# Six output tiles instead of four side by side in the first projection of a two-layer encoder step

## Chip, cores and metric

One Trainium2 chip, one core. The metric is device microseconds of one execution; of several runs the median counts.

## What is computed

One inference step of a two-layer streaming encoder, for 256 new frames of a prompt and 32 of a running stream, which the kernel keeps side by side as T = 288 columns. Layer 0 mixes tokens with a gated linear recurrence, layer 1 with differential attention; a gated convolutional MLP follows each. The change lies in layer 0's first part:

```python
def rglru_mixer(x, conv_hist, h0, w_in, conv_w, conv_b, gate_w, gate_b, log_lam, w_out):
    u = x @ w_in                                   # x is the RMS-normed input, 2048 wide; w_in 2048 x 4096
    gate_br, rec = u[..., :D_RNN], u[..., D_RNN:]
    y = jax.nn.gelu(gate_br)
    full = jnp.concatenate([conv_hist, rec], axis=1)
    xc = causal_dwconv(full, conv_w, conv_b, t)    # width 4
    g = sigmoid(einsum('btnc,ncd->btnd', xc.reshape(bsz, t, 16, 128), gate_w) + gate_b)
    r, i = g[..., :128], g[..., 128:]
    log_a = -8.0 * r * softplus(-log_lam)
    a, mult = exp(log_a), sqrt(-expm1(2.0 * log_a))
    h = linear_recurrence(a, mult * i * xc, h0)    # h[t] = a[t] * h[t-1] + b[t]
    return (h * y) @ w_out
```

## The kernel before, in words

Everything is fp32 and transposed: channels on the 128 partitions, the 288 columns along the free axis. A product of fp32 accuracy is made of three matmuls: high half of the weights by high half of the input (L926), high weights by low input (L927), low weights by high input (L928). ScalarE (ACT) makes each high half by a copy (weights L809, x L144), VectorE (DVE) each low half by a subtraction (weights L814, x L147). One 128-row chunk of one output tile is a triplet of such matmuls. Weights are streamed from HBM once.

The work is a list of units. A unit is some consecutive chunks (2, 4 or 8) of one output tile's weights: one load, one cut into halves, then its triplets. `phase(tiles, group)` (L224) orders the units of a stage: the first `group` tiles advance side by side, unit by unit, the rest come one after another. The first projection (L705 to L712) has 32 tiles: r0 to r15 feed the recurrence, g0 to g15 the gelu gate, in the order r0 r1 g0 g1 r2 r3, then r4 r5 g2 g3, r6 r7 g4 g5 and so on. Tiles with n below 2, which are the four of the group, are cut into units of 2, 2, 4 and 8 chunks, all others into 8 and 8. So units 0 to 3 need chunks 0 and 1 of x, units 4 to 7 chunks 2 and 3, units 8 to 11 chunks 4 to 7, units 12 to 15 chunks 8 to 15.

The order of the work on every engine is written out by the loop at L898, one step for each unit i: it loads units up to i + 5 (L804, on SyncE's queue SP), lets ACT cut unit i + 3 (four buffers, so this cut waits until TensorE has finished unit i - 1), runs all pending jobs that are due at i (`S.run_due`, L906), lets DVE write the low half of unit i + 3, and issues unit i's matmuls. Jobs due at the same step run in the order in which they were put on the list. All engines work their own instructions in order.

Before the loop, SP is given the constants (L856), the first twelve unit loads and the 16 x tiles, one transfer for each, in between (L857 to L862). Splits of later x tiles (L883), squares (L885), the norm row (L887) and other loads are jobs with due steps. The norm row (`norm_row`, L196) sums the squares by two matmuls with a matrix of ones: L198 for the sum that GpSimd (POOL) built (L167), L199 for the one that DVE built (L163). DVE then makes 1/sqrt by iteration (L176 to L191). Every tile's result waits for this row.

When a tile of the first projection is finished, its `rec_done` (L283) or `gate_done` (L376) puts a chain of jobs on the list:

- r tiles: s1 loads the raw gate weights (L274), copies three history columns (POOL, L291), scales the sums out of PSUM (DVE, L294 and L295) and applies the first tap (ACT, L297); s2 the other three taps (DVE, L304); s3 and s4 split the result and the gate weights (ACT L309 and L140, DVE L141 and L314); s6 the six gate matmuls (L326 to L328); s7 sigmoids and tanh (ACT, L334 to L339) and a product (POOL, L340); s8 a reciprocal (DVE, L343) and a product (POOL, L344); s9 a copy (L348). After each second tile, s10 takes square roots for both (ACT L357, products on POOL L358), and s11 runs the recurrence as two scans (DVE, L364 and L366).
- g tiles: scale (DVE, L207), gelu (ACT, L386), product with h (POOL, L389), split into Hh and Hl (L392, L395).

A stage's due step is the chain's base plus a lag. Before, the base is the tile's last unit i (i + 1 for r0 and r1) and a small extra w delays s6 and later for r0 to r3 (L350 to L373). Gelu, sqrt and the sigmoid and tanh pair use different ACT tables, each change of which is an ACT_TABLE_LOAD.

PSUM: four banks rotate among the tiles, a pair of banks (`psS`) serves the gates of even r tiles, two more (`psA`) the gates of odd ones and the norm.

## Time and profile before

| | us |
|---|---|
| median of 3 runs (2511.88 to 2512.2) | 2511.97 |
| the profiled execution | 2512.42 |
| its span, first to last instruction | 2510.6 |
| TensorE matmul busy (share of the span) | 2480.7 (99%) |
| VectorE busy | 1633.6 (65%) |
| ScalarE busy | 1198.4 (48%) |
| GpSimd busy | 282.7 (11%) |

Busy times are sums over the span; the engine names PE, PEld (weight load), DVE, ACT, POOL and SP are those of the profile. A row of a list in order of time gives the start, the duration, the engine, the source line, the operation, output and inputs with shapes, and in brackets the idle time before it with what ended it. The time of a matmul in the profile is a modelled one that overlaps the next matmul's; the distance between starts is the pace. The first projection runs from 5 to about 220 us.

### The profile page before, as it was taken

How to read it: one execution, taken by the hardware profiler on the slowest of the kernel's cores; microseconds unless marked ns; L12 is line 12 of the kernel's file. 1: busy time of each engine (PE TensorE's matmuls, PEld its weight loads, DVE VectorE, ACT ScalarE, POOL GpSimd, SP SyncE). 2: the span in 40 equal slices, each digit the busy share in tenths (PEclk: the TensorE clock that was granted, in tenths of full speed). 3: DMA queues.
4: the chain of work that ended last, by engine and by line, in shares of the span. 5: the costliest groups of instructions: out<-in, count | busy, mean ns of one | idle time of the engine just before them, and what ended most of it. 6: DMA issues, size and time to landing. Idle time of an engine off the chain costs nothing.

```text
span 2510.6 us, 46015 instructions
## 1 busy us (share of the span) xinstructions
PE 2480.7 (99%) x18556; PEld 2472.7 (98%) x18556; DVE 1633.6 (65%) x2599; ACT 1198.4 (48%) x1756; POOL 282.7 (11%) x779
## 2 busy tenths in 40 slices
PE   8999999999999999999999999999999999999997
PEld 7999999999999999999999999999999999999997
DVE  7987666666446666555677677766666446666544
ACT  6887444444334444444445444544444334444442
POOL 3554110000000000011000000210000000000011
PEclk9999999999999999999999999999999999999999
DMA  6444544445554444555554553544445554444553
GB/s 218 160 167 164 170 160 168 163 166 161 164 167 166 166 167 162 160 168 171 181 163 160 177 170 116 193 162 166 165 163 161 166 169 168 162 167 166 162 164 113
DMA packets 126934, 414.36 MB, mean 165 GB/s; under 512 B 14336, under 2 KB 24192, under 8 KB 126720
## 3 DMA queue, kind: packets, MB, share of 16 engines
q1 hardware_dynamic: 126288, 411.17, 49.8%
q8 instruction: 145, 2.38, 0.4%
q14 instruction: 69, 0.57, 0.1%
q10 hardware_dynamic: 432, 0.25, 0.0%
HBM read 403.86 MB, written 7.50 MB: 164 GB/s over the span
## 4 chain that ended last, share of the span: by engine, by line
PE 97%; DVE 1%; DMA 0%; issue 0%; ACT 0%; SPq 0%; DVEq 0%; ACTq 0%
PE acc L926 32%; PE acc L928 31%; PE acc L927 31%; DVE x L936 0%; DVE wl L814 0%; PE os_ps L653 0%; DMA wr<-w_in 0%; DMA x<-x 0%; PE spare L926 0%; PE gate_ps L327 0%; PE gate_ps L328 0%; PE spare L928 0%; PE spare L927 0%; PE gate_ps L326 0%; PE osq_ps L682 0%
## 5 line engine op out<-in xcount | busy, mean ns | idle before, releaser
L809 ACT ACTIVATE wh<-wr 128x1024 fp32r<-128x1024 f32 (+2 forms) x776 | 799.2, 1030 | 1206.2 <-PE acc L927 848.7
L814 DVE TENSOR_TENSOR wl<-wr,wh 128x1024 fp32r<-128x1024 f32 (+2 forms) x776 | 925.9, 1194 | 510.6 <-ACT wh L809 510.0
L926 PE MATMUL acc<-xh,wh 128*128 128x288 f32 x4096 | 1217.3, 297 | 5.0 <-ACT xh L144 5.0
L928 PE MATMUL acc<-xh,wl 128*128 128x288 f32 x4096 | 1206.4, 295 | 5.5 <-DVE wl L814 5.4
L927 PE MATMUL acc<-xl,wh 128*128 128x288 f32 x4096 | 1209.7, 295 | 0.0
L928 PEld LDWEIGHTS acc<-xh,wl 128*128 128x128 f32 x4096 | 772.3, 189 | 7.0 <-DVE wl L814 6.9
L926 PEld LDWEIGHTS acc<-xh,wh 128*128 128x128 f32 x4096 | 768.9, 188 | 5.7 <-ACT xh L144 5.0
L927 PEld LDWEIGHTS acc<-xl,wh 128*128 128x128 f32 x4096 | 770.1, 188 | 0.9 <-DVE xl L147 0.3
L927 PE MATMUL acc<-Hl,wh 128*128 128x288 f32 x1504 | 443.9, 295 | 0.8 <-DVE Hl L395 0.8
L926 PE MATMUL acc<-Hh,wh 128*128 128x288 f32 x1504 | 444.3, 295 | 0.0
L928 PE MATMUL acc<-Hh,wl 128*128 128x288 f32 x1504 | 442.9, 294 | 0.0
L927 PEld LDWEIGHTS acc<-Hl,wh 128*128 128x128 f32 x1504 | 282.3, 188 | 1.3 <-DVE Hl L395 1.3
L928 PEld LDWEIGHTS acc<-Hh,wl 128*128 128x128 f32 x1504 | 283.0, 188 | 0.0
L926 PEld LDWEIGHTS acc<-Hh,wh 128*128 128x128 f32 x1504 | 281.8, 187 | 0.1
L437 DVE SCALAR_TENSOR_TENSOR c<-up,cff,c 128x290 f32<-128x290 f32 x352 | 182.6, 519 | 6.2
L431 POOL COPY st_ff<-up 128x2 f32<-128x2 f32 x176 | 34.6, 197 | 1339.1 <-DVE up L427 1339.1
L426 DVE TENSOR_TENSOR up<-acc,rb 128x32 f32<-128x32 f32 x176 | 33.7, 191 | 128.7 <-PE acc L928 128.7
L926 PE MATMUL acc<-Hhx,wh 128*128 128x288 f32 x384 | 113.7, 296 | 0.0
L927 PE MATMUL acc<-Hlx,wh 128*128 128x288 f32 x384 | 113.3, 295 | 0.0
L928 PE MATMUL acc<-Hhx,wl 128*128 128x288 f32 x384 | 112.9, 294 | 0.0
L429 ACT ACTIVATE c<-up,cff 128x290 f32<-128x290 f32 x176 | 108.6, 617 | 0.7 <-DVE up L427 0.7
L167 POOL TENSOR_TENSOR ssq<-ssq,sq 128x288 f32<-128x288 f32 x63 | 70.1, 1113 | 288.9 <-ACT sq L154 288.4
(211 smaller groups left out, 1651.3 us busy)
## 6 DMA issues: line engine op xcount, KB each, us to landing
wr<-w_up SPq DMA_DIRECT2D x352, 512.0 KB, 3.7
wr<-w_dn SPq DMA_DIRECT2D x128, 448.0 KB, 3.3
wr<-w_qkv SPq DMA_DIRECT2D x96, 512.0 KB, 4.2
wr<-w_dn SPq DMA_DIRECT2D x64, 512.0 KB, 3.6
wr<-w_in SPq DMA_DIRECT2D x60, 512.0 KB, 3.9
wr<-w_rg_out SPq DMA_DIRECT2D x32, 512.0 KB, 3.7
wr<-w_at_out SPq DMA_DIRECT2D x24, 512.0 KB, 4.0
wr<-w_at_out SPq DMA_DIRECT2D x16, 256.0 KB, 3.1
```

Of the source, the lines that this page charges most:

```text
L167: nc.gpsimd.tensor_add(acc_box["a"], acc_box["a"], sq)
L426: nc.vector.tensor_mul(buf[:, 2:34], ps[:, 0:NS], rb[:, 0:NS])
L429: nc.scalar.activation(c, buf[:, 0:UP_N], AF.Identity, scale=ff(f"w{l}", f), bias=ff(f"b{l}", f))
L431: nc.gpsimd.tensor_copy(st_ff[:, f, 0, :], buf[:, 290:292])
L437: nc.vector.scalar_tensor_tensor(c, buf[:, t:t + UP_N], ff(f"w{l}", t * 2 * NF + f), c, op0=OP.mult, op1=OP.add)
L809: nc.scalar.activation(u["wh"][:, :n], u["raw"][:, :n], AF.Copy)
L814: nc.vector.tensor_sub(u["wl"][:, :n], u["raw"][:, :n], r32(u["wh"])[:, :n])
L926: nc.tensor.matmul(o, wh, h, start=u["first"] and z == 0, stop=False)
L927: nc.tensor.matmul(o, wh, lo, start=False, stop=False)
L928: nc.tensor.matmul(o, wl, h, start=False, stop=u["last"] and z == nk - 1)
```

## The change

- `FIRST = 6`: the six tiles r0 r1 g0 g1 r2 r3 advance side by side, all cut into 2, 2, 4 and 8. Units 0 to 5 need x chunks 0 and 1, units 6 to 11 chunks 2 and 3, units 12 to 17 chunks 4 to 7, units 18 to 23 chunks 8 to 15. Tiles 4 and 5 (r2, r3) accumulate in the two banks of `psS` (`bank` 0 and 1 of L913 to L919).
- x is loaded in eight transfers of two tiles each; the first 16 columns of the constants are loaded first, the rest after the second x pair; 16 units are loaded before the loop instead of 12.
- The coefficients (`coef`) become a job of step 8; splits, squares and the norm row move to later steps; so do the side loads, lambda and the state output.
- The chains of r0 to r5 get bases 21, 22, 23, 25, 25, 29 and extra lags w of 1, 2, 3, 3, 4, 2; for r2 to r5 s3 and s4 are delayed by w too.
- Buffers: three raw gate buffers instead of two, five `xc` and five `y` instead of four.

```diff
+FIRST = 6
-        raw = rgp.tile([P, 256], F32, tag="gwr", name="gwr")
+        raw = rgp.tile([P, 256], F32, tag="gwr", name="gwr", bufs=3)
-                e["xc"] = rgp.tile([P, REC_N], F32, tag="xc", name="xc", bufs=4)
+                e["xc"] = rgp.tile([P, REC_N], F32, tag="xc", name="xc", bufs=5)
-            w = (1, 2, 1, 1)[n] if n < 4 else 0
-            stages = [(1, s1), (2, s2), (3, s3), (4, s4)]
+            w = (1, 2, 3, 3, 4, 2)[n] if n < 6 else 0
+            v = w if n > 1 else 0
+            stages = [(1, s1), (2, s2), (3 + v, s3), (4 + v, s4)]
             stages += [(t + w, f) for t, f in ((6, s6), (7, s7), (8, s8), (9, s9))]
-            S.chain(i + (1 if n < 2 else 0), *stages)
+            S.chain((21, 22, 23, 25, 25, 29)[n] if n < 6 else i, *stages)
-                e["y"] = rgp.tile([P, T], F32, tag="y", name="y", bufs=4)
+                e["y"] = rgp.tile([P, T], F32, tag="y", name="y", bufs=5)
-    tiles = [tile_units(d["w_in"], n + (KC if w == "r" else 0), 0, [8, 8] if n >= 2 else [2, 2, 4, 8],
-                        xh, xl, need_of("n0"), rec_done(n) if w == "r" else gate_done(n))
-             for w, n in order]
-    phase(tiles, 4)
+    tiles = [tile_units(d["w_in"], n + (KC if w == "r" else 0), 0, [8, 8] if t >= FIRST else [2, 2, 4, 8],
+                        xh, xl, need_of("n0"), rec_done(n) if w == "r" else gate_done(n),
+                        t - 4 if t in (4, 5) else None)
+             for t, (w, n) in enumerate(order)]
+    phase(tiles, FIRST)
-    def load_x(a, b):
-        for c in range(a, b):
-            nc.sync.dma_start(x[c], d["x"][c // 2][:, (c % 2) * T:(c % 2 + 1) * T])
+    def load_x(*pairs):
+        for c in pairs:
+            nc.sync.dma_start(xx[c], d["x"][c])
-    nc.sync.dma_start(crg, d["p_rg"])
-    for i in range(12):
-        tag = "hs" if i < 4 else "y"
-        load(units[i], rgp.tile([P, T], F32, tag=tag, name="w0", bufs=4) if i < 8 else None)
-        if i in (0, 4, 8):
-            load_x(i // 2, max(i, 2))
-    load_x(8, KC)
+    nc.sync.dma_start(crg[:, 0:KC], d["p_rg"][:, 0:KC])
+    for i in range(16):
+        raw = None
+        if i < 2 * FIRST:
+            tag, n = (("hs", T), ("y", T), ("a", REC_N))[i // 4]
+            raw = rgp.tile([P, n], F32, tag=tag, name="w0", bufs=5 if tag == "y" else 4)
+        load(units[i], raw)
+        if i == 0:
+            load_x(0)
+        elif i == FIRST - 1:
+            load_x(1)
+            nc.sync.dma_start(crg[:, KC:], d["p_rg"][:, KC:])
+        elif i == 2 * FIRST - 1:
+            load_x(2, 3)
+    load_x(4, 5, 6, 7)
-    coef()
+    S.at(8, coef)
-    for t, c, n in ((1, 2, 2), (3, 4, 2), (5, 6, 2), (7, 8, 4), (8, 12, 4)):
+    for t, c, n in ((3, 2, 2), (9, 4, 2), (10, 6, 2), (14, 8, 4), (16, 12, 4)):
         S.at(t, lambda c=c, n=n: split_x(c, c + n))
-    for t, c, n in ((9, 0, 4), (10, 4, 4), (11, 8, 4), (12, 12, 4)):
+    for t, c, n in ((17, 0, 4), (18, 4, 4), (19, 8, 4), (20, 12, 4)):
         S.at(t, lambda c=c, n=n: square_x(c, c + n))
-    S.at(14, lambda: norm_row("n0"))
-    S.at(24, side_loads)
-    S.at(40, lam_setup)
+    S.at(21, lambda: norm_row("n0"))
+    S.at(28, side_loads)
+    S.at(44, lam_setup)
-    S.at(72 + 14, rg_states)
+    S.at(2 * 2 * KC + 2 * FIRST + 14, rg_states)
-    dma_ptr, cut_ptr = 12, 4
+    dma_ptr, cut_ptr = 16, 4
```

## Rows read from the trace of the kernel before

**Rows 1.** The page, parts 1 and 2: busy time of the engines, and TensorE's granted clock

```profile
PE 2480.7 (99%) x18556; PEld 2472.7 (98%) x18556; DVE 1633.6 (65%) x2599; ACT 1198.4 (48%) x1756; POOL 282.7 (11%) x779
PEclk9999999999999999999999999999999999999999
```

**Rows 2.** The list of waits, TensorE, 0 to 140 us (total, times, longest)

```profile
PE acc L928 <- DVE wl L814: 5.4, 5, 2.3
```

**Rows 3.** Groups of instructions, 0 to 11.3 us, then the timeline, TensorE

```profile
L926 PE MATMUL acc<-xh,wh 128*128 128x288 f32 x8 | 3.7, 463 | 5.0 <-ACT xh L144 5.0
...
11.32 0.35 PE L926 MATMUL acc<-xh,wh 128*128 128x288 f32 x1
...
33.09 0.29 PE L928 MATMUL acc<-xh,wl 128*128 128x288 f32 x1
33.95 0.75 PE L198 MATMUL ssq_ps<-ssq,ones 128*128 128x288 f32 x2 [0.56 <-POOL ssq L167]
...
36.09 0.29 PE L928 MATMUL acc<-xh,wl 128*128 128x288 f32 x1
...
36.49 0.29 PE L928 MATMUL acc<-xh,wl 128*128 128x288 f32 x1
```

**Rows 4.** Busy time by stretch (PE, PEld, DVE, ACT, POOL, PEclk, DMA share, GB/s)

```profile
0.00:4.97 4.97, 0.00 (x1) 0.01 (x1) 0.61 (x3) 2.23 (x3) 1.27 (x8) 1.00 0.55 147
4.97:13.00 8.03, 8.03 (x37) 7.67 (x38) 4.01 (x10) 4.31 (x12) 4.03 (x16) 1.00 0.89 261
13.00:20.00 7.00, 5.81 (x41) 5.34 (x41) 6.80 (x15) 6.85 (x16) 2.82 (x8) 1.00 0.97 310
```

**Rows 5.** Transfers issued in 0 to 40 us (count, size, median us to landing)

```profile
x<-x SPq DMA_DIRECT2D x16, 144.0 KB, 3.9
wr<-w_in SPq DMA_DIRECT2D x4, 256.0 KB, 5.4
```

**Rows 6.** The timeline, DVE and TensorE, 53 to 118 us

```profile
53.57 1.63 DVE L304 SCALAR_TENSOR_TENSOR xc<-rec,crg,xc 128x292 f32<-128x292 f32 x3
...
101.75 2.74 DVE L304 SCALAR_TENSOR_TENSOR xc<-rec,crg,xc 128x292 f32<-128x292 f32 x3 [0.16 <-ACT xc L297]
...
104.41 1.22 DVE L814 TENSOR_TENSOR wl<-wr,wh 128x1024 fp32r<-128x1024 f32 x1
...
105.68 0.40 PE L928 MATMUL acc<-xh,wl 128*128 128x288 f32 x1 [0.91 <-DVE wl L814]
...
117.50 0.41 PE L327 MATMUL gate_ps<-xcl,gwh 128*128 128x292 f32 x1 [1.13 <-DVE xcl L314]
```

**Rows 7.** The timeline, ACT, 4 to 6 us

```profile
4.38 0.53 ACT L144 ACTIVATE xh<-x,crg 128x288 fp32r<-128x288 f32 x1 [0.18 <-DMA x<-x]
...
5.21 0.53 ACT L144 ACTIVATE xh<-x,crg 128x288 fp32r<-128x288 f32 x1 [0.30 <-DMA x<-x]
```

**Rows 8.** Groups of instructions, DVE, 0 to 240 us

```profile
L163 DVE TENSOR_TENSOR ssq<-ssq,sq 128x288 f32<-128x288 f32 x7 | 6.3, 896 | 0.7 <-ACT sq L154 0.4
```

**Rows 9.** The timeline, ACT, 122 to 130 us

```profile
122.61 1.28 ACT L334 ACT_TABLE_LOAD   x1
123.90 0.51 ACT L334 ACTIVATE r<-gate_ps,crg 128x292 f32<-128x292 f32 x1
...
125.61 0.43 ACT L348 ACTIVATE a<-q 128x292 f32<-128x292 f32 x1
...
128.10 1.04 ACT L809 ACTIVATE wh<-wr 128x1024 fp32r<-128x1024 f32 x1
129.06 0.76 ACT L392 ACTIVATE Hh<-y 128x288 fp32r<-128x288 f32 x2
129.72 1.04 ACT L809 ACTIVATE wh<-wr 128x1024 fp32r<-128x1024 f32 x1
```

**Rows 10.** What ACT's line 297 waited for, 40 to 240 us (us, times)

```profile
  POOL rec L291: 7.9, 4
```

**Rows 11.** Busy time by stretch, columns as in rows 4

```profile
80.00:100.00 20.00, 20.00 (x152) 20.00 (x152) 17.42 (x21) 19.37 (x34) 12.62 (x13) 1.00 0.42 143
```

## The prediction

> **What bounds the kernel now.** I read the page's totals first: TensorE (PE) is busy for 99% of a 2510.6 us span [rows 1], so time can only come from stretches where PE waits. Next the list of PE's waits over the first 140 us: five waits for the low half of a weight tile lead it with 5.4 us [rows 2]. These figures count idle time after a matmul's modelled end, so they are short. Start to start is better: three matmuls (a triplet, one 128-row chunk of one output tile) start every 0.40 us (36.09 to 36.49), and the first eight triplets ran slowly, until 11.32 [rows 3]. From there to the norm's matmul at 33.95 there is work for 48 - 8 = 40 triplets, 16.0 us, and 22.63 went by: **6.6 us lost**. Of these, 0.73 is the gap from 33.09 to 33.95 less one matmul's 0.13; the other 5.9 belong to loads and cuts. The DMA engines were 89%, then 97% busy at 261 and 310 GB/s from 4.97 to 20 [rows 4]: with four tiles side by side each x tile feeds only four weight chunks, and x, 16 x 144 KB, competes with weights [rows 5].
>
> Later, past 100 us, PE loses a little more: 0.91 before 105.68, waiting for a weight's low half that VectorE (DVE) wrote at 104.41 behind a long convolution, and 1.13 before 117.50, where a gate matmul waits for DVE [rows 6]. Start to start each costs 0.27 more (0.17 as at the norm, where 0.56 idle were 0.73, and 0.1 for the longer matmul after it): **2.6 us**. The reader should see that in this stretch ScalarE (ACT) and DVE set the pace, not DMA.
>
> **The change part by part.** *Six tiles.* PE's work is unchanged, its order is not. Each of the first x tiles now feeds six weight chunks. Before, x and the weights of four tiles, 2.4 + 4.2 MB, are wanted in 64 x 0.40 = 25.6 us, 256 GB/s; now 2.4 + 6.3 MB in 38.4 us, 225 GB/s, under the rates shown [rows 4, 5]. The slow opening still ends near 11.3 (eight triplets). Then units 4 and 5 end at 12.9, units 6 to 11 at 17.7, 12 to 17 at 27.3, 18 to 20 at 36.9. Bytes ahead of x's chunks 4 to 7 are 2.9 MB and of chunks 8 to 15 5.1 MB; by 13 us 2.8 MB, by 20 us 5.0 MB had moved before (0.73 + 2.10 + 2.17) [rows 4]. They are wanted at 17.7 and 27.3, so 4 to 7 us of margin. **The 5.9 go, less 0.2** for units 12 and 13, where ACT has two cuts of half a large tile and four x tiles (0.53 each) in a row [rows 7]; bounds 0 and 1 for that.
>
> *x in pairs, small first part of the constants.* Ahead of the first matmul stood 121 + 128 + 144 KB; now 8 + 128 + 288 (sizes by the code's shapes). That is 31 KB more, 0.1 us at 261 GB/s [rows 4]. Bounds: -0.4 (the constants' 113 KB) and +0.8 (the second x tile was taken up 0.8 us after the first [rows 7]). I take **+0.1**. SP issues 8 x loads in place of 16 and one more for the constants, 7 issues fewer; nothing is later for that, since the transfers, not their issue, end last. The coefficients' 16-column steps move to step 8, behind a cut needed three units later; they are wanted only in step 29: nothing.
>
> *Squares and norm row.* The squares are in steps 17 to 20, the norm row in step 21, one step after the last squares instead of two. ACT: the load of unit 16 can be issued only when unit 12's cut frees its buffer, about 16.8, and takes some 4 us (5.4 among the crowded first ones [rows 5]); ACT then has steps 13 to 16, two half-size cuts, two large, eight x tiles, 6.6 us, and reaches the first square's step at 27.4. DVE ends the previous low halves near 29.2 and has until the last sum a copy 0.3, seven sums of 0.9 and three low halves of 1.2: 10.2 us [rows 6, 8]. The second norm matmul so starts at 39.4; PE could have started it 0.6 after 36.9. The wait is 1.9 instead of 0.73: **+1.2** (bounds -0.7, no wait, and +2.8, if GpSimd (POOL) slows each sum as it slowed the convolution).
>
> *Chains later.* Nothing is computed more or less; r0 to r5 start when the norm row exists, and r6 and r7 keep their times. So the gates of r2 to r7 fall into ten steps, 33 to 42. I count ACT there, start to start: 10 cuts x 0.96 = 9.6; 6 gate stages x 1.71 = 10.3; nine table loads x 1.29 = 11.6, because gates, roots and gelus need different tables; and 29 short operations, most of them 0.33 (the pair of H copies took 0.66 to the next start): 6 copies, 6 roots, 3 first taps (0.5), 6 split halves, 4 gelus, 4 H copies, 10.2 [rows 9]. **41.7 us, in steps where PE needs 10 x 3.2 + 5 gates x 0.8 = 36.** In the most crowded ten steps of before, 24 to 33, the same count (four gate stages, five loads) gives 31.8 against 35.2, and behind them 2.6 were lost. ACT is in order, so behind each late gate stage stand the next cut and the next split: DVE's low half waits for the cut, PE for both. ACT also waited for POOL's 3-column copy, 7.9 us in four cases [rows 10], because that copy is queued behind POOL's products, and r6's and r7's copies now stand behind the roots' products of r1 and r2's. Walking the queues with these durations, from PE's start of step 33 as zero: ACT leaves step 33 at 6.3 (two table loads), step 34 only at 14 (r6's tap waits for POOL until 13.5), step 35 at 18.4, and splits r6 at 22; DVE, after r7's rows, a low half, r4's reciprocal and an H half, writes r6's low half at 26.7. PE reaches r6's gates in step 39, at 21.6, and waits 5.0; the next unit waits behind it. By the same walk r7's gates in step 41 wait 3.1. Bounds: 0.7, the 5.7 excess less a lead of some 5 us that a cut has over its use; and 5.7 + three POOL waits of 2.0 each = 11.7. Between the two I go by the row nearest, the 2.6 that a less crowded stretch already lost, plus half of the excess, 2.9: **5.5 where 2.6 stood, +2.9**.
>
> *Buffers.* A third raw gate buffer covers the five steps between r2's load and its split; without it SP would hold the weight loads behind it. r2 and r3 accumulate in the pair of banks that r0's gates take in step 28; they are emptied in steps 24 and 26, two steps (6.4 us) ahead: nothing. r4's split in step 32 must wait for r2's gate matmuls at the head of that step, under 1 us on ACT, in the walk. Side loads, lambda and state output move by four steps, off PE's path: nothing.
>
> **Sum:** -5.9 + 0.2 + 0.1 + 1.2 + 2.9 = -1.5 against the profiled execution's 2512.42 (its span and 1.8 around it, which the change leaves), so 2510.9; that run lies 0.45 above the median of 2511.97, so **2510.5**. 0.2%, about what a measurement of this kernel can tell from no change, is 5.0 us: faster means under 2507.0, slower over 2517.0.
>
> **The rivals.** *Everything is hidden* (faster): ACT's lead and the later starts absorb the excess, only 0.7 is lost in the chains: -5.9 + 0.2 + 0.1 + 1.2 - 1.9 = -6.3, 2505.7. For it: from 80 to 100 us ACT was busy for 19.4 of 20 us and PE lost nothing [rows 11]. Against: ACT must find 5.7 us that it hasn't. It decides if the PE waits between 80 and 160 us sum to under 2. *The gates choke* (slower): the place is r6's and r7's gate matmuls and the cuts between; price, the upper bound of 11.7 instead of 2.6, and the squares then also at their upper bound because POOL and DVE slow one another, as the three taps show with 1.63 alone and 2.74 beside POOL [rows 6]: -5.9 + 0.2 + 0.1 + 2.8 + 9.1 = +6.3, 2518.3. It decides once chain waits pass 13 us with the squares as forecast. *The loads stay late*: if the pairs land no sooner than the singles and the cuts of unit 12 on still wait, half of the 5.9 stays: -1.5 + 2.9 = +1.4, 2513.4. Against: the margins above.
>
> *The clock.* PE's longest wait for a low half was 2.3 us [rows 2], and the granted clock stays at its upper level, 9 or more tenths in every slice [rows 1]; the walk has a longer gap, 5.0 us. By those rows a gap costs only itself. If a longer one dropped the clock to its lower level, the opening shows a price: eight triplets of matmuls that took 0.46 each in place of 0.29 used the time to 11.32 [rows 3], though the clock reads 9 there too; at twice 0.40 such eight cost 3.2 us more, -1.5 + 3.2 = +1.7, 2513.7. The Trainium skill (TensorE: Matmul & The Clock Gate, HAM oscillation) states that a long enough wait between bursts returns the clock to half rate; no run here shows it, and by that rule the time would be the 2513.7 just given.
>
> **How the numbers follow.** Forecast, between the cases, 2507 to 2515 alone: 0.40. All hidden: 0.36. Choked: 0.15. Loads stay late: 0.05. Clock: 0.04. Faster: the hidden case and the low edge of the forecast, 0.39. Slower: the choked case and a little of the forecast, 0.16. Same: 0.45. The range reaches to the hidden case with half of the norm row's extra taken off, 2504.8, and to just under the choked case, 2517.
>
> **What would show it.** Right: no wait for wl between 11 and 30 us; a wait of 1 to 3 us before the second norm matmul, near 39; PE waits between 85 and 160 us that sum to 3 to 9 and stand at gate matmuls of r6 and r7 or at cuts in steps 36 to 43, with ACT near full and table loads between its gate stages. Wrong: waits at DMA before 30 us; no wait in the chains; or waits past step 48.

## The result, and the profile after

The changed kernel took 2526.95 us (median of 4 runs, 2524.92 to 2527.86) against 2512.09 for the kernel before: ratio 1.0057, interval 1.0045 to 1.0069. It is 15 us slower, more than the 0.2% that can be told apart, and above the predicted range of 2504.8 to 2517 us. Its profiled execution took 2527.3 us, 14.9 more than that of before.

The page's first part and the list of TensorE's waits in 0 to 165 us (total us, times, longest) answer to [rows 1, 2]:

```profile
PE 2484.5 (98%) x18556; PEld 2476.4 (98%) x18556; DVE 1638.5 (65%) x2603; ACT 1200.3 (48%) x1761; POOL 276.7 (11%) x779
...
PE gate_ps L328 <- DVE xcl L315: 7.3, 4, 3.4
PE acc L938 <- ACT xh L145: 5.3, 1, 5.3
PE gate_ps L327 <- ACT r L335: 3.4, 1, 3.4
PE ssq_ps L199 <- POOL ssq L168: 3.1, 1, 3.1
PE spare L940 <- DVE wl L818: 2.3, 1, 2.3
PE acc L940 <- DVE wl L818: 1.6, 1, 1.6
```

Lines have moved by up to 12: L926 to L928 are now L938 to L940, the gate matmuls L327 to L329. PE's busy time grew by 3.8 us although it does the same matmuls, and the waits at gates, 1.1 us before, are 10.7. The timeline of TensorE shows where they stand; each pair is the last start before a gap and the first after it, and of the last three gaps only the start behind it is shown (answers to [rows 3, 6]):

```profile
25.80 0.29 PE L939 MATMUL spare<-xl,wh 128*128 128x288 f32 x1
28.43 0.40 PE L940 MATMUL spare<-xh,wl 128*128 128x288 f32 x1 [2.34 <-DVE wl L818]
...
39.32 0.29 PE L940 MATMUL acc<-xh,wl 128*128 128x288 f32 x1
42.69 0.75 PE L199 MATMUL ssq_ps<-ssq,ones 128*128 128x288 f32 x2 [3.07 <-POOL ssq L168]
...
43.94 0.80 PE L938 MATMUL acc<-xh,wh 128*128 128x288 f32 x1
...
100.77 0.29 PE L940 MATMUL acc<-xh,wl 128*128 128x288 f32 x1
104.49 0.40 PE L327 MATMUL gate_ps<-xch,gwh 128*128 128x292 f32 x1 [3.43 <-ACT r L335]
...
113.32 0.30 PE L327 MATMUL gate_ps<-xch,gwh 128*128 128x292 f32 x1
115.27 0.40 PE L328 MATMUL gate_ps<-xcl,gwh 128*128 128x292 f32 x1 [1.65 <-DVE xcl L315]
...
122.44 0.30 PE L327 MATMUL gate_ps<-xch,gwh 128*128 128x292 f32 x1
126.09 0.61 PE L328 MATMUL gate_ps<-xcl,gwh 128*128 128x292 f32 x1 [3.35 <-DVE xcl L315]
...
146.28 0.40 PE L940 MATMUL acc<-xh,wl 128*128 128x288 f32 x1 [1.56 <-DVE wl L818]
...
151.39 0.40 PE L328 MATMUL gate_ps<-xcl,gwh 128*128 128x292 f32 x1 [1.78 <-DVE xcl L315]
...
159.37 0.40 PE L328 MATMUL gate_ps<-xcl,gwh 128*128 128x292 f32 x1 [0.51 <-DVE xcl L315]
```

In the load stage one large wait for a weight's low half is left, 28.43. The norm row waits 3.37 us from start to start. From 100 us on there are gaps at the gates of r5 (step 37), r6 (39) and r7 (41), then at a cut (146.28) and at the gates of r8 and r9 (151.39 and 159.37). The same stretches in TensorE's table by stretch (PE busy and starts, granted clock, DMA share, GB/s):

```profile
44.00:46.00 2.00, 2.00 (x10) 0.50 0.44 156
46.00:48.00 2.00, 2.00 (x12) 0.65 0.85 282
48.00:52.00 4.00, 4.00 (x32) 1.00 0.13 40
104.00:108.00 4.00, 3.51 (x17) 0.68 0.38 131
126.00:128.00 2.00, 1.91 (x8) 0.50 0.00 0
```

Behind three gaps the granted clock fell to its lower level (0.50 is 1.2 GHz, 1.00 is 2.4) for part of a stretch or all of it, and matmuls started every 0.24 to 0.27 us instead of 0.133; behind the other gaps it held. Summed over the slow starts behind each gap, that cost 1.7 us at the norm, 1.7 behind r5's gates and 1.5 behind r7's.

So the 14.9 us are, within 0.1: the gaps past 100 us, start to start less one matmul's 0.13, 3.59 + 1.82 + 3.52 + 1.71 + 1.95 + 0.68 = 13.3, where 2.6 stood before (+10.7); the slow pace, +5.0; and the start with the norm row's gap, -0.9 (behind the norm row PE had its 72 triplets done at 43.94; before, 48 were done at 35.20, and 24 more at 0.40 make that 44.8).

What holds r5's gates is seen on ACT and POOL, in steps 34 and 35 (timelines):

```profile
96.13 0.79 ACT L360 ACTIVATE t<-t 128x292 f32<-128x292 f32 x2
101.04 0.63 ACT L298 ACTIVATE xc<-rec,crg 128x292 f32<-128x292 f32 x1 [4.13 <-POOL rec L292]
...
102.64 1.28 ACT L335 ACT_TABLE_LOAD   x1
103.93 0.50 ACT L335 ACTIVATE r<-gate_ps,crg 128x292 f32<-128x292 f32 x1
```

```profile
97.31 0.81 POOL L345 TENSOR_TENSOR ip<-ip,q 128x292 f32<-128x292 f32 x1 [4.50 <-DVE q L344]
98.09 2.79 POOL L361 TENSOR_TENSOR ip<-ip,t 128x292 f32<-128x292 f32 x2
100.83 0.18 POOL L292 COPY rec<-crg 128x3 f32<-128x3 f32 x1
```

```profile
94.85 0.43 DVE L142 TENSOR_TENSOR gwl<-gwr,gwh 128x256 fp32r<-128x256 f32 x1 [3.89 <-ACT gwh L141]
95.19 1.97 DVE L344 RECIPROCAL q<-q 128x292 f32<-128x292 f32 x1
```

r5's gates need the two PSUM places that r3's sigmoid still has to read (103.93). ACT comes to it late, because ahead of it in its queue r6's first tap waited 4.13 us for POOL's copy of three columns, which stood behind products of other tiles. Those in turn waited for DVE's reciprocal, and DVE had stood idle 3.89 us for ACT's split of gate weights, to which ACT came only after working without a pause from 86.57. So at r5 the three engines hold each other up by turns. DVE's own table by stretch:

```profile
70.00:80.00 10.00, 5.99 (x9) 1.00 0.58 196
80.00:90.00 10.00, 9.92 (x13) 1.00 0.32 105
90.00:100.00 10.00, 6.11 (x7) 1.00 0.35 120
100.00:120.00 20.00, 15.97 (x22) 0.91 0.28 93
120.00:160.00 40.00, 37.05 (x53) 0.96 0.37 127
```

DVE stands idle for 4 us in 70 to 80 and again in 90 to 100 and is then 93% busy from 120 to 160; before, it had 27.0 of the 30 us from 70 to 100 filled. The two longest idle times end with ACT's split of gate weights, at 73.95 (3.25 us) and 94.85 (3.89). Ahead of the first ACT had itself waited for TensorE to reach the step (2.95 us before 72.22): that work was due late. Ahead of the second ACT was full.

### The profile page after: what moved, and what is told of

Its sections match the earlier page's. It is cut to its first block, busy times and chain, and to the rows that moved or that the text cites. A ratio compares the mean times of both kernels' runs of the same rounds, so it can differ in the third digit from the quotient of the medians.

```text
span 2525.5 us, 46023 instructions
## 1 busy us (share of the span) xinstructions
PE 2484.5 (98%) x18556; PEld 2476.4 (98%) x18556; DVE 1638.5 (65%) x2603; ACT 1200.3 (48%) x1761; POOL 276.7 (11%) x779
## 4 chain that ended last, share of the span: by engine, by line
PE 95%; DVE 3%; ACT 1%; issue 1%; POOL 0%; DMA 0%; DVEq 0%; SPq 0%; ACTq 0%; POOLq 0%
PE acc L938 31%; PE acc L940 30%; PE acc L939 30%; DVE wl L818 1%; ACT wh L813 0%; PE spare L940 0%; PE spare L938 0%; DVE q L344 0%; PE spare L939 0%; DVE x L948 0%; DMA wr<-w_in 0%; PE os_ps L656 0%; DVE hs L369 0%; DVE Hl L398 0%; PE osq_ps L685 0%
## 5 line engine op out<-in xcount | busy, mean ns | idle before, releaser
L938 PE MATMUL acc<-xh,wh 128*128 128x288 f32 x4064 | 1209.4, 298 | 5.3 <-ACT xh L145 5.3
L940 PE MATMUL acc<-xh,wl 128*128 128x288 f32 x4064 | 1197.5, 295 | 1.6 <-DVE wl L818 1.6
L938 PEld LDWEIGHTS acc<-xh,wh 128*128 128x128 f32 x4064 | 764.0, 188 | 5.9 <-ACT xh L145 5.3
L940 PEld LDWEIGHTS acc<-xh,wl 128*128 128x128 f32 x4064 | 767.8, 189 | 2.0 <-DVE wl L818 2.0
L938 PE MATMUL acc<-Hh,wh 128*128 128x288 f32 x1504 | 444.4, 295 | 0.0
L940 PE MATMUL acc<-Hh,wl 128*128 128x288 f32 x1504 | 442.9, 294 | 0.0
L940 PEld LDWEIGHTS acc<-Hh,wl 128*128 128x128 f32 x1504 | 283.1, 188 | 0.0
L938 PEld LDWEIGHTS acc<-Hh,wh 128*128 128x128 f32 x1504 | 281.9, 187 | 0.1
L938 PE MATMUL acc<-Hhx,wh 128*128 128x288 f32 x384 | 113.7, 296 | 0.0
L940 PE MATMUL acc<-Hhx,wl 128*128 128x288 f32 x384 | 112.9, 294 | 0.0
```

The source lines that it names most:

```text
L938: nc.tensor.matmul(o, wh, h, start=u["first"] and z == 0, stop=False)
L940: nc.tensor.matmul(o, wl, h, start=False, stop=u["last"] and z == nk - 1)
```

## The experiments

The theories: (a) the norm row's wait was mis-sized; (b) the clock, not the gaps, costs; (c) the chains' stages are due too late and then too densely, for vector time or for ACT. Numbers in the headings are the runs' order; each list of waits covers 46 to 165 us and counts idle time after a matmul's modelled end. Single runs of one kernel lie up to 3 us apart, so a difference of 2 us between two medians is not clear of noise by itself.

One difference comes ahead of every chain. In the profiled executions of runs 3, 5 and 7 the clock fell behind the load stage's gap and not behind the norm row; in the changed kernel it was the other way round. The first norm matmul starts at 42.3 to 43.1 us in all four, but r0's gates start at 66.8, 66.2 and 66.9 us instead of 68.1. So 1.2 to 1.9 us of the gains of these three profiled executions are there before the chains, where their edits act.

### 1. Filler matmuls ahead of three waits

```diff
 def norm_row(key):
     ps = psA.tile([P, 512], F32, tag="A", name="ssq_ps")
+    if key == "n0":
+        for z in range(18):
+            nc.tensor.matmul(ps[:, :T], xh[z % 8][:, 0:P], xh[z % 8], start=True, stop=True)
...
+                if n in (5, 7):
+                    for z in range(18):
+                        nc.tensor.matmul(acc[:, :T], zero, xh[z % 8], start=False, stop=False)
```

> The changed kernel (2526.95 us) with 18 multiplications more on PE ahead of each of three long waits: the norm row's first matmul (gap 3.37 us between two starts), r5's gates (3.72) and r7's gates (3.65). At the 0.133 us of the neighbouring matmuls they fill 2.4 us of each gap and add nothing to the result. Theory 'clock': the stretches behind these three gaps had a granted clock of 0.50 to 0.89 and cost about 1.7 us each; with gaps of 1.0 to 1.3 us left the granted clock stays at 1.00 there, the waits themselves last as long as before, and the time is 2521 to 2523 us. Rival 'other cause': the slow pace behind the gaps comes with the work that follows, the granted clock falls all the same, time 2526 to 2529 us.

Measured: 2526.16 us, ratio 1.0057 (1.0042 to 1.0072). TensorE's stretches behind the norm row and behind r6's gates, which had no filler:

```profile
44.00:48.00 4.00, 4.00 (x32) 1.00 0.62 201
...
112.00:116.00 4.00, 2.63 (x11) 0.56 0.30 92
```

The clock held at both filled waits that were long (norm row, r5), so the slow pace does belong to the gaps. But the time is the rival's: PE was early at r6's gates, waited 3.2 us there instead of 1.7 and ran slowly behind that (0.56), and behind r8's gates once more. The slow pace in this run sums to 4.4 us, hardly less than the 5.0 of the changed kernel. The fall is a price of its own, but sparing it in two places moved the wait and the fall to others.

### 2. The squares earlier

```diff
-    for t, c, n in ((17, 0, 4), (18, 4, 4), (19, 8, 4), (20, 12, 4)):
-        S.at(t, lambda c=c, n=n: square_x(c, c + n))
+    for t, cs in ((12, (1, 3, 5, 7)), (14, (0, 2)), (17, (4, 6, 8, 9, 10, 11)), (18, (12, 13, 14, 15))):
+        S.at(t, lambda cs=cs: square_x(*cs))
```

> The changed kernel with the squares for the norm spread otherwise: chunks 1, 3, 5, 7 in step 12, chunks 0 and 2 in step 14, six in step 17 and the last four in step 18, where the change had four each in steps 17 to 20. Theory 'norm row mis-sized': the wait of 3.1 us at the norm row's first matmul goes, with the slow clock behind it (about 1.7), and all later waits are as they were: 2521 to 2523.5 us. Rival 'fixed by the chains': what is gained there is waited for again at the gates of r5 to r7, since ACT, DVE and POOL are then as late as before: 2525 to 2528 us.

Measured: 2523.21 us, ratio 1.0043 (1.0028 to 1.0058), as theory (a) says: -3.7. The norm row's wait is gone, the waits at gates are not (12.2 us in the list, 12.3 in the changed kernel's).

### 3. The history copies on DVE

```diff
-                nc.gpsimd.tensor_copy(buf[:, 0:3], rg("hist", 3 * n, 3))
+                nc.vector.tensor_copy(buf[:, 0:3], rg("hist", 3 * n, 3))
```

> The changed kernel with one edit: the copy of three history columns into the recurrence buffer goes from POOL to DVE, 16 copies in all. In the changed kernel ACT waited 4.13 us at 96.9 us for such a copy, which stood on POOL behind two products of another tile. Theory 'copy': r6's convolution then starts 3 to 3.5 us earlier, r3's sigmoid with it, and r5's gates find their PSUM places read: that wait (3.4) and its slow clock (1.7) go, and the two waits behind it (1.7 and 3.4) get smaller: 2516 to 2521.5 us. Rival 'ACT is full': ACT has as much to do before the sigmoid, it is late by its own work, the waits stay within 1 us of what they were: 2525 to 2528 us.

Measured: 2524.72 us, ratio 1.0052 (1.0035 to 1.0069): between the two ranges. r5's wait is gone, as the copy theory says; r6's grew from 1.7 to 5.1 us, and a cut behind it waits 3.1. The gain of 2.2 us is not clear of noise, the single runs overlap (2523.74 to 2526.70 against 2524.92 to 2527.86); the places of the waits are. The copy was the last link at r5, and DVE's queue was the next.

### 4. No table loads

This kernel leaves gelu and the square root out of the computation, and with them most changes of ACT's table: 3 loads from 46 to 165 us instead of 16.

```diff
-                nc.scalar.activation(e["y"], e["y"], AF.Gelu_apprx_tanh)
+                nc.scalar.activation(e["y"], e["y"], AF.Tanh)
-                        nc.scalar.activation(u["t"], u["t"], AF.Sqrt, scale=4.0)
+                        nc.scalar.activation(u["t"], u["t"], AF.Tanh, scale=4.0)
```

> The changed kernel with the Gelu of the gate tiles and the square root of the recurrence both replaced by Tanh, so that these two functions are left out of the computation, and with them the table loads between 85 and 165 us (1.28 us each, some twelve). Theory 'ACT is full': with 15 us of loads gone ACT is early, and the waits at the gates of r5, r6 and r7 and their slow clock go: 2512 to 2517 us. Theory 'copy': ACT still waits for POOL's small copy, whose products come from DVE's reciprocals and not from ACT's loads, but the one load between that copy and r3's sigmoid is gone: r5's wait shrinks by 1.3 to 2.6 us and no more: 2519 to 2525 us.

Measured: 2521.21 us, ratio 1.0035 (1.002 to 1.0051), in the range of the copy theory, though r5's wait went altogether. 7.5 us of waits stay, all for DVE (xcl 4.5, wl 3.0). Without ACT's loads the kernel gains 5.7 us, so ACT has a part in the loss; it is not the whole of it.

### 5. No reciprocal

This kernel leaves the recurrence's reciprocal out; a short multiplication stands in its place.

```diff
-                nc.vector.reciprocal(e["q"], e["q"])
+                nc.vector.tensor_scalar(e["q"], e["q"], 0.5, None, op0=OP.mult)
```

> The changed kernel with the reciprocal of the recurrence left out: DVE multiplies the same tile by 0.5 in its place (16 times; 1.96 us each before, some 0.4 after). Theory 'DVE is the bound': between the norm row and r9's gates DVE was busy 90 per cent and more in most stretches of ten microseconds, and every wait at a gate ended with an instruction of DVE or with ACT behind one; with 10 reciprocals of 1.5 us less before r9's gates, the waits at the gates of r5 to r9 (about 13 us) and the two falls of the clock in them go: 2512 to 2516 us. Rival 'ACT and POOL in turn': it is the order in which the three engines wait for each other, and the next of them holds r5 to r7 as long: 2520 to 2526 us.

Measured: 2519.22 us, ratio 1.003 (1.0018 to 1.0042). A miss for both: the gain of 7.7 (up to 1.9 of it ahead of the chains) is the largest of any one edit, but 6.7 us of waits stay. r5's gates still wait 1.8 for r3's sigmoid, ahead of which ACT waited 2.46 us for POOL's copy. Taking vector time away removed about half of the waits; that the rest is the order in which the engines wait for each other is argued from the chain at r5 and not shown.

### 6. Norm row and chains earlier

```diff
-    S.at(21, lambda: norm_row("n0"))
+    S.at(19, lambda: norm_row("n0"))
-            w = (1, 2, 3, 3, 4, 2)[n] if n < 6 else 0
+            w = (1, 2, 2, 3, 3, 3)[n] if n < 6 else 0
-            S.chain((21, 22, 23, 25, 25, 29)[n] if n < 6 else i, *stages)
+            S.chain((19, 20, 22, 23, 25, 27)[n] if n < 6 else i, *stages)
```

(and the squares of run 2)

> The changed kernel with the squares spread as in the second run (2523.21 us with that alone), the norm row in step 19 instead of 21, and the chains of r0 to r5 begun 1 to 2 steps earlier (gates in steps 26, 28, 30, 32, 34, 36 instead of 28, 30, 32, 34, 35, 37); r6 and later as they were. Theory 'DVE has too little time': the work of six tiles, which waits for the norm row, has to be done beside the rest; DVE stood idle about 8 us between 70 and 100 us because the stages were due late, and then was full. With the stages due earlier that idle time is used, and the waits at r5 to r9 shrink by 5 to 9 us: 2513 to 2518 us. Rival 'crowding': chains begun closer to the norm row wait there instead, at r0 to r3, and the time stays at 2521 to 2526 us.

Measured: 2528.87 us, ratio 1.0068 (1.0051 to 1.0085), above both ranges. The attempt spoilt its own start: the norm row in step 19 waited 5.9 us for the sums, and r2's first stage, put ahead of the last unit of the head, held that unit for 4.8, because r2 and r3 share one PSUM buffer. Behind that the chains wait 5.7 us instead of 12.3; whether for the earlier stages or for the 11 us of delay, run 8 asks.

### 7. Two subtractions on POOL

```diff
-                nc.vector.tensor_sub(Hl[n], e["y"], r32(Hh[n]))
+                nc.gpsimd.tensor_sub(Hl[n], e["y"], r32(Hh[n]))
-        split(hi, lo, gws[n])
+        nc.scalar.activation(hi, gws[n], AF.Copy)
+        nc.gpsimd.tensor_sub(lo, gws[n], r32(hi))
```

> The changed kernel with two subtractions of each tile moved from DVE to POOL: the low part of the gate weights (0.43 to 0.97 us on DVE) and the low part of the first projection's output (0.39 to 1.07), 32 in all. Theory 'DVE is the bound': about 10 us less on DVE before r9's gates, POOL was busy about half of that time; the waits fall by 4 to 8 us: 2519 to 2523 us. Rival 'POOL is in the way': DVE's instructions beside POOL's last longer (the recurrence's small scan took 0.18 or 0.83 us), and ACT waits for POOL's history copy behind more work: 2526 to 2532 us.

Measured: 2524.61 us, ratio 1.0052 (1.0037 to 1.0067): -2.3, the waits 9.7 instead of 12.3. 1.6 us short of the first theory's range, and below the second's: the waits fell by 2.6 where 4 to 8 were expected. The gain in time is not clear of noise (single runs from 2524.09 to 2526.32, the changed kernel's from 2524.92).

### 8. The chains earlier, the norm row left in step 21

```diff
-            w = (1, 2, 3, 3, 4, 2)[n] if n < 6 else 0
+            w = (0, 0, 1, 2, 3, 3)[n] if n < 6 else 0
-            S.chain((21, 22, 23, 25, 25, 29)[n] if n < 6 else i, *stages)
+            S.chain((21, 22, 23, 24, 25, 27)[n] if n < 6 else i, *stages)
```

(and the squares of run 2)

> The second run (squares spread, norm row in step 21; 2523.21 us) with the chains of r0 to r5 due earlier: gates in steps 27, 28, 30, 32, 34 and 36 where the change has 28, 30, 32, 34, 35 and 37; r6 and later as they were. r2's first stage stays behind the last matmul of the head, since both tiles of the spare pair are one buffer (the sixth run waited 4.8 us for that, and 5.9 us at a norm row in step 19). Theory 'due too late': the waits at the gates of r5 to r9 were 14 us together in the second run and were 7 in the sixth, where only the start was spoilt; they come to 5 to 8 us here with one fall of the clock instead of two: 2513 to 2518 us. Rival 'the engines in turn': the sixth run's chains had few waits only because PE had been held up 11 us before; without that they wait as in the second run: 2521 to 2526 us.

Measured: 2517.12 us, ratio 1.0021 (1.0012 to 1.003), 6.1 below run 2 and in the range of "due too late". The waits fall from 12.2 to 7.4, with one fall of the clock. DVE's table by stretch, to be laid beside that of the changed kernel:

```profile
70.00:80.00 10.00, 7.59 (x9) 1.00 0.36 121
80.00:90.00 10.00, 10.00 (x11) 1.00 0.43 143
90.00:100.00 10.00, 8.51 (x13) 1.00 0.46 147
```

DVE does 26.1 us of work in these 30, where the changed kernel did 22.0.

### 9 and 10. What adds nothing

Run 9 adds the edits of runs 3 and 7 to run 8.

> The eighth run's kernel with the two edits of the third and the seventh run added: the history copies on DVE, and the two subtractions of each tile on POOL; each gained 2.2 to 2.3 us on the changed kernel alone. Theory 'vector work': both act on the engines that end the waits, and what is left of them shrinks by 2 to 4 us more: 2510 to 2515 us. Rival 'the gains were the same microseconds': the two edits and the earlier chains take away the same waits, so nothing adds up: within 1 us of the eighth run.

Measured: 2516.84 us, ratio 1.0019 (1.001 to 1.0029): level with run 8 within the spread, as the rival says.

Run 10 is run 2 with this:

```diff
+        elif i < 14:
+            raw = (lamb.rearrange("p a b -> p (a b)"), cff)[i - 12]
     load_x(4, 5, 6, 7)
+    load(units[16])
+    load(units[17])
```

> The second run's kernel (2523.21 us) with units 12 and 13 loaded into two constant buffers that stand empty until step 28, and units 16 and 17 therefore loaded without waiting for unit 12's cut. Theory 'the load stall is real time': the gap of 2.4 us at 25.6 us (and the 1.2 us near 36) goes, and the whole rest moves up by 2 to 3.5 us: 2519.5 to 2521.5 us. Rival 'paid for again': the squares and the norm row are then the later ones, PE waits 2 us there, and the time stays at 2522.5 to 2524.5 us.

Measured: 2522.98 us, ratio 1.0044 (1.0029 to 1.0059). The gap at 25.6 us is gone, yet r0's gates come only 0.2 us earlier (63.5 against 63.7), so the rival holds; 1.6 us of the 3.0 us that run 2 waited for low halves up to 46 us are left, and where the rest is paid was not followed.

### 11 and 12. r6 and r7 later, the lambda work out of the way

```diff
-            w = (0, 0, 1, 2, 3, 3)[n] if n < 6 else 0
+            w = (0, 0, 1, 2, 3, 3, 2, 2)[n] if n < 8 else 0
-    S.at(44, lam_setup)
+    S.at(90, lam_setup)
```

(run 8 with this and the copies of run 3; run 12 adds the loads of run 10; the lambda work is a job for layer 1 that stood in the middle of these chains)

> The eighth run's kernel (2517.12 us) with three edits: the chains of r6 and r7 two steps later from their third stage on (gates in steps 41 and 43, so that five steps lie between r5's and r6's gates), the history copies on DVE (ACT waited 4.3 us for one at 94.7 us in the eighth run), and the lambda work in step 90, behind this stage, where ACT waited 4.6 us for DVE in the changed kernel. Theory 'due too late, then too dense': the 8 us of waits at the cuts and gates of r5 to r8 in the eighth run and the one fall of the clock shrink to 2 to 4 us: 2510 to 2513.5 us, no slower than the kernel before. Rival 'vector time': DVE is full from 80 us on, what is taken from r6 and r7 is waited for at r8 and r9: 2515 to 2518 us.

> The eleventh run's kernel with the load edit of the tenth added (units 12 and 13 in two buffers that stand empty until step 28, units 16 and 17 loaded without waiting for a cut). In the tenth run it took the gap of 2.4 us at 25.6 us away and gained nothing, behind it the chains waited as long. Theory 'paid for again at the chains': with the chains no longer the limit the gap's time shows: 1 to 2.5 us faster than the eleventh run. Rival 'paid for again before the chains': x and the weights' cuts come no sooner in sum, PE waits a little at several cuts instead of once: within 0.7 us of the eleventh run.

Measured: 2515.86 (1.0015, 1.0006 to 1.0024) and 2514.77 us (1.001, 1.0001 to 1.0019). Run 11 falls in the range of its rival, vector time: 7.6 us of waits, 7.4 in run 8, now at cuts as well. The load edit is now worth 1.1, the low end of its first theory, but the single runs of 12 (2514.50 to 2515.37) lie within those of 11 (2514.45 to 2517.20), so this is not shown.

### 13 and 14. Work taken off DVE

Run 13 is run 12 with the history copies back on POOL, but right behind the taps that free the buffer, and Hl on POOL; run 14 adds the gate weights' low half on POOL (both as in run 7).

```diff
             def s2():
                 for t in range(1, 4):
                     nc.vector.scalar_tensor_tensor(e["xc"], buf[:, t:t + REC_N], rg("cw", t * KC + n),
                                                    e["xc"], op0=OP.mult, op1=OP.add)
+                if n + 2 < KC:
+                    nc.gpsimd.tensor_copy(buf[:, 0:3], rg("hist", 3 * n + 6, 3))
```

> The twelfth run's kernel (2514.77 us) with the history copies back on POOL but issued early (right behind the convolution that frees the buffer, seven or more steps before they are needed), and the low part of the first projection's output on POOL. Theory 'vector time': DVE was busy 9.9 of 10 us from 80 to 110 us in the twelfth run; by its rows 0.15 to 0.77 us for each copy and 0.4 to 0.45 for each subtraction come off it, some 3 to 4 us before r6's gates, and the waits there (four, 6.2 us, and the fall of the clock behind them) shrink by as much: 2510.5 to 2512.5 us, level with the kernel before. Rival 'price of six': the waits move to another instruction and the time stays at 2514 to 2516 us.

> The thirteenth run's kernel with the low part of the gate weights on POOL too (0.42 to 1.04 us each on DVE). Theory 'vector time': DVE loses 4 us more before r6's gates; 0.5 to 2 us faster than the thirteenth run, 2509 to 2512 us. Rival 'POOL in the chain': POOL's subtraction comes behind its products, a gate waits for it as one did in the ninth run (1.1 us), and the time is level with the thirteenth run or up to 1.5 us more.

Measured: 2513.23 (1.0004, 0.9995 to 1.0013) and 2510.61 us (0.9995, 0.9986 to 1.0004). In that order, as vector time says; run 13 a little above its range, run 14 in it. No single run of 12 (from 2514.50) is as fast as the slowest of 13 or 14 (2514.32 and 2512.70), and run 14 differs from 13 by 16 subtractions taken off DVE alone, with ACT's work the same: here vector work is shown to cost time. The list of TensorE's waits of run 14, and DVE's table:

```profile
PE acc L948 <- DVE wl L820: 2.1, 1, 2.1
PE gate_ps L330 <- DVE xcl L317: 1.9, 1, 1.9
```

```profile
70.00:80.00 10.00, 9.93 (x10) 1.00 0.35 121
80.00:90.00 10.00, 9.28 (x8) 1.00 0.54 172
90.00:100.00 10.00, 9.93 (x13) 1.00 0.36 120
```

Waits of 4.0 us are left, no slow stretch behind them, and DVE fills 29.1 of the 30 us.

### 15 and 16. Is it the six tiles, and are two waits left to save?

Run 15 makes the four DVE edits of run 14 (early copies, two subtractions on POOL, lambda work in step 90) in the kernel before. Run 16 is run 14 with `(0, 0, 1, 2, 3, 3, 3, 3)`.

> The kernel before (2512.1 us), four tiles side by side and its own squares, loads and due steps, with the four edits that take work off DVE or away from this stage: the history copies early, the two subtractions of each tile on POOL, the lambda work in step 90. Theory 'six tiles gain at the start': the kernel before waits only 2 to 2.6 us in its chains, so these edits give it 0.5 to 2.5 us and no more: 2509.5 to 2511.6 us, level with the fourteenth run (2510.6); six tiles then bring some 5 us at the start and hand back as much to the later chains. Rival 'six tiles bring nothing': 2507 to 2509.5 us, better than the fourteenth run.

> The fourteenth run's kernel (2510.61 us) with the chains of r6 and r7 one step later from their third stage on (gates in steps 42 and 44 instead of 41 and 43). Theory 'due steps': the wait at r6's gates (1.9 us) goes and nothing takes its place: 2508 to 2509.8 us. Theory 'vector time': DVE does the same work in the same order but for one step, the wait of 2.1 us for a weight's cut near 107 us stays, and r8 or the cuts behind get what r6 is spared: 2509.8 to 2512 us.

Measured: 2515.78 (1.0012, 1.0004 to 1.0021) and 2511.96 us (0.9999, 0.999 to 1.0008). Run 15 meets neither range: what saves the changed kernel time costs the kernel before 3.5 us. The load stage is not the place: its gap, to 26.43, is 3.15 us from start to start, and the clock fell behind it (1.6 us), but r0's gates start at 54.72 us, before at 54.77. The loss stands in the chains: 3.4 us of waits instead of 2.0, and a slow pace behind r7's gates (118.97) that costs 1.6. By the last r gates this kernel is 3.0 us late (229.2 against 226.2). Why less work on DVE makes these waits longer was not followed; but run 14's time does not come from the DVE edits alone. Run 16 is vector time again: r6's wait went, r8 and r9 wait 1.4 together, the cut near 107 us still 2.1.

The runs side by side (list of waits 46 to 165 us, time):

| kernel | waits | us |
|---|---|---|
| changed | 12.3 | 2526.95 |
| 2 squares | 12.2 | 2523.21 |
| 8 chains earlier | 7.4 | 2517.12 |
| 11, 12: r6 and r7 later, loads | 7.6, 6.2 | 2515.86, 2514.77 |
| 13 | 5.2 | 2513.23 |
| 14 | 4.0 | 2510.61 |
| before | 2.0 | 2512.09 |

Run 14 waits 2.0 us longer in the chains than the kernel before, yet its last r gates start 2.7 us earlier (223.5 against 226.2): by this sum six tiles, with the squares and loads mended, gain some 4.7 us at the start, and the chains take part of it back. The norm row gives about the same, 4.4 us: in run 14 its matmuls end, with 72 triplets done, at 40.4 us, where the kernel before would have needed the 44.8 worked out above. None of the runs was faster than the kernel before by more than the measurement can tell.

## Why the prediction was wrong

The forecast was -1.5 us, the result +14.9. Term by term:

- **Loads and start, -5.9 + 0.2 + 0.1: measured about -3.4.** The early waits for low halves went, and the slow opening ended at 10.8, not 11.3. But where 0.2 was forecast, with a bound of 1, a gap of 2.5 stayed (2.63 less 0.13). The step that failed is the one in the squares' part that lets one load come late, unit 16's at 20.8. It came at 21.6, and unit 17's, which no step had, at 24.88; ACT waited for both (timeline):

```profile
21.60 0.63 ACT L813 ACTIVATE wh<-wr 128x512 fp32r<-128x512 f32 x1 [2.81 <-DMA wr<-w_in]
24.88 0.63 ACT L813 ACTIVATE wh<-wr 128x512 fp32r<-128x512 f32 x1 [2.64 <-DMA wr<-w_in]
```

  The gap of 2.63 at 28.43 is their effect: in run 10, where these two loads wait for no cut, it is gone. The value of -3.4 is the -0.9 of the start less the next term.
- **Norm row, "The wait is 1.9 instead of 0.73: +1.2": measured 3.24, +2.5.** The squares began at 31.67, not 27.4, behind those two late loads. The sum that came last was also another than forecast: TensorE waited 3.07 us for POOL's sum at the first norm matmul (42.69), where the working had DVE's sum at the second. The size is inside the bounds; run 2 showed the term by taking it away.
- **Chains, "the row nearest ... +2.9": measured +10.7.** This is the step that failed most: going by "the row nearest" instead of by the walk. The hand walk had found r6's and r7's gates and 8.1 us there (measured 1.82 + 3.52), and POOL's copies as a link; it was set aside for the 2.6 of a less crowded stretch plus half an excess. r5's wait of 3.59 was not in the walk: it has r6's tap wait for POOL, but not that r3's sigmoid stands behind this tap and that r5's gates need what the sigmoid reads. The upper bound of 11.7 (13.3 measured) was near the truth. The count was also made for ACT alone. Run 4 took ACT's table loads away and kept 7.5 us of waits, all for DVE; run 5 took DVE's reciprocal away and kept 6.7. By these two ACT and DVE weigh about the same. Run 8 showed the due steps (7.4 us of waits where 12.2 stood), and runs 13 and 14 vector work on top of that (5.2 and 4.0). What was not counted is DVE, and that work which is due later leaves it idle first (8 us in 70 to 100) and is then missing time.
- **Clock, "By those rows a gap costs only itself": measured +5.0.** Gaps up to 2.60 start to start, all that the trace of before held, did cost only themselves there; three of 3.4 to 3.7 did not. The rival's price for one fall, 3.2, was too high for these three (1.5 to 1.7; the dearest, in run 12, was 2.8), its chance of 0.04 far too low, and it was thought of as one event.

The choked rival named the direction, and its sign of over 13 us of chain waits came, just (13.3). Its place holds in part: 5.3 of the 13.3 stand at the gates of r6 and r7, none at a cut between them, 3.6 at r5 and 4.3 at a later cut and at r8 and r9. Two of the signs that were named for "wrong" or against "right" came too: a wait for wl before 30 us, and one past step 48 (r9's gates, step 49). For 2527 the rival's 2518.3 also lacked the slow clock and the late loads.

## What to carry to other kernels

When a common event on which many chains wait is moved later, count the work behind it for every engine from the event to the point where the steady state is reached again, and look for idle time in front of the crowded stretch: stages due too late waste it. Where a walk through the queues by hand gives a larger wait than a row from an easier stretch, do not set the walk aside: here it was the better forecast. Price a gap of a tensor engine that the trace has not shown yet with the slow pace behind it.

## What the runs showed of the hardware

**The fall of the clock is not settled by the length of the gap.** In run 2 the gap at r5's gates was as long as in the changed kernel, 3.72 us (96.39 to 100.11); behind it the clock held, and it fell behind the next gap of 3.49 (to 110.91). The gap of 2.63 in the load stage cost nothing behind it in the changed kernel and 1.6 us in run 3. At r8's gates a gap of 2.08 us cost nothing in the changed kernel (to 151.39, clock 1.00) and 1.6 us in run 1 (to 149.53, clock 0.63). In run 16 the clock fell behind one of 2.40 (106.99 to 109.39):

```profile
100.00:104.00 4.00, 3.89 (x29) 1.00 0.43 131
112.00:116.00 4.00, 4.00 (x21) 0.57 0.17 47
```

```profile
108.00:112.00 4.00, 2.62 (x16) 0.86 0.36 111
112.00:116.00 4.00, 4.00 (x24) 0.72 0.36 120
```

Gaps of 2.1 to 3.7 us went both ways; what decides beside their length stays open. What a fall costs in the end depends on what follows: run 3's slow 1.6 us in the load stage were made good at the norm row, where TensorE then waited 1.86 us from start to start instead of 3.37. The Trainium skill (TensorE: Matmul & The Clock Gate, HAM oscillation) states that a long enough wait between bursts returns the clock to half rate; the three falls of the changed kernel agree with it, while run 2's 3.72 and run 16's 2.40 show that the order of lengths alone does not forecast it.

**DVE beside POOL.** The same scan of 32 columns took 0.18 us alone and 0.83 while POOL multiplied (timelines of run 8):

```profile
90.00 0.83 DVE L367 TENSOR_TENSOR_SCAN hs<-a,crg,ip 128x32 f32<-128x32 f32 x1
95.37 0.18 DVE L367 TENSOR_TENSOR_SCAN hs<-a,crg,ip 128x32 f32<-128x32 f32 x1
```

```profile
88.00 2.75 POOL L361 TENSOR_TENSOR ip<-ip,t 128x292 f32<-128x292 f32 x2
```

The low half of r's split took 0.45 us alone and 1.07 beside POOL's products in the changed kernel (89.38 and 99.13), that of the gate weights 0.42 or 1.03 in run 8, so vector time in a crowded stretch is longer than the sum of its instructions alone. The Trainium skill (SBUF — State Buffer, SBUF: two separate sides) states that the two engines hold a shared pair of ports in turn, each for a whole instruction, when DVE's has two inputs in SBUF; these rows agree. It may also be why moving work from DVE to POOL gave little in run 7 (2.3 us); no run shows that.
